# Expert down matrices loaded with two or three neighbouring rows for each partition, in a two-layer decoder trunk

## The chip, the cores and the metric

One core of one Trainium2 chip. The metric is the device time of one execution in microseconds, lower is better; the kernel is timed several times and the median is shown.

## The reference

A trunk of two layers on 256 tokens of width 1024, all in fp32. Layer 0 has differential attention beside a short convolution, then a dense SwiGLU; layer 1 has a gated spatial mix, then experts. Only the experts matter here: each token goes to the two of eight experts that its router picks.

```python
def moe_swiglu(h, router_w, w1, w3, w2):
    ...
    logits = jnp.einsum('nd,de->ne', xt, router_w, preferred_element_type=jnp.float32)
    top_val, top_idx = lax.top_k(logits, TOP_K)
    gates = jax.nn.softmax(top_val, axis=-1)
    ...
        return (jax.nn.silu(xb @ w1[e]) * (xb @ w3[e])) @ w2[e]
    ...
    contrib = y_sorted * gate_flat[order][:, None].astype(h.dtype)
    out = jax.ops.segment_sum(contrib, sorted_token, num_segments=n_tok)
```

`w1[e]` and `w3[e]` are 1024 x 2816 (the up matrices), `w2[e]` is 2816 x 1024 (the down matrix). All eight experts' matrices are read once: 277 MB of the 358 MB that the kernel reads.

## The kernel before

**Weights.** `Stream` brings every weight matrix through one chain, in one order. SP issues loads into raw tiles of 128 partitions x 3072 fp32 (1536 KB, 12 KB for each partition); in the expert stage there are seven (`RAWA` + `RAWB`). `convert` then splits each raw tile, mostly 1536 columns at a time: ACT rounds it to `whi` (L153) and DVE takes the rest, `wlo = raw - whi` (L154). There are four pairs of these conversion buffers. TensorE (PE) multiplies from them: a product is `whi` and `wlo` each against the activations. Once both halves of a raw tile are converted, the next load may go into it. `prefetch` issues loads as soon as a raw tile can be had, so SP waits for DVE to be done with L154.

**What a load looks like.** `rows` packs blocks of 128 matrix rows into raw tiles, and `piece` writes the source of a load of m blocks as `(k p) f -> p k f`: partition p gets row p of each block, so its m rows lie 128 rows apart in the matrix, and each is a run of 4 KB for a width of 1024.

**An expert step.** For each expert the 2816 hidden columns go in three steps (`MAIN`: 1024, 1024 and 768 wide). `up` multiplies the gathered tokens with the step's columns of `w1` and `w3`. Then the hidden values, which lie with tokens on the partitions, must be turned so that hidden columns lie on the partitions, in blocks of 128. `down` multiplies block j with the rows of `w2` of that block; it is held back by one step, so that it runs beside the next step's `up`.

- Experts in the places 0, 2, 4, 6 hold up to 128 tokens ("large"). `up` leaves the product in `g`, written by DVE in two halves (L1160), and `turn` transposes it block by block (L1195): each transpose loads 128 columns of `g` into PE as weights and streams the identity, out to `gTp`.
- Experts in the places 1, 3, 5, 7 hold up to 64 ("small"): the rounded tokens sit in 64 lanes and their remainders in the other 64. `up` leaves two tiles `ab`, for `w1` and `w3`, written by ACT in two halves (L1151). `folded` turns a block and adds both lanes at once (L1175): it loads 128 columns of `ab` as weights and streams `fold`, 64 columns; fp32 matmuls of this kind run in two passes. Silu and product come after.

**Order.** On ACT and DVE the order of the expert stage is written out in the program; on PE a scheduler interleaves `down`, transposes, folds and the next `up`.

In the functions below, `g` is what `up` returned, `s` the step, `ctxs[e]["small"]` tells the two kinds apart. `set_aside` loads one raw tile's three blocks as three loads into spare buffers, before the stage has its seven tiles. A second stream (`st2`, `stream.fixed`) serves tokens over an expert's room; its loads bring one block each, and it doesn't run here.

Of the kernel before, what the change touches and what calls it, by code (L numbers as in the profile page):

```python
# [21 lines left out]
P = 128  # L22
D = 1024
# [3 lines left out]
HALF = 64  # L27
# [13 lines left out]
def first_of(parts):  # L41
    return parts[0][0]


def wide(parts):
    return sum(w for _, w in parts)


class Stream:
# [3 lines left out]
    def __init__(self, nc, raws, cvs, cols=RAWC, fixed=None):  # L53
        self.nc, self.raws, self.cvs, self.cols, self.fixed = nc, raws, cvs, cols, fixed
        self.specs, self.loaded, self.n_load = [], [], 0
        self.chunks, self.ready, self.n_conv = [], [], 0
        self.cur, self.pos, self.n_use = None, 0, 0
        self.spare = {}
        self.base, self.ahead, self.parts, self.stop = 0, len(cvs), 1, None

    def add(self, parts, lens):
        i = len(self.specs)
        self.specs.append(parts)
        off = 0
        for n in lens:
            self.chunks.append((i, off, n))
            off += n

    def rows(self, units, cut=0):


        total = sum(u[3] for u in units)
        room = total % self.cols or self.cols
        i = 0
        while i < len(units):
            j, n = i, 0
            while j < len(units) and n < room:
                n += units[j][3]
                j += 1
            assert n == room  # L80
            parts, off, a = [], 0, i
            while a < j:
                b = a + 1
                while b < j and units[b][0] is units[a][0] and units[b][2:] == units[a][2:] \
                        and units[b][1] == units[b - 1][1] + 1:
                    b += 1
                w, k, c0, n1 = units[a]
                parts.append((off, n1, b - a, self.piece(w, k, b - a, c0, n1)))
                off += n1 * (b - a)
                a = b  # L90
            m, q, u = -(-room // CVC), room // 512, 512
            if cut and j == len(units):
                m = cut
            if room % 512:
                q, u = room // 384, 384
            self.add(parts, [(q // m + (x < q % m)) * u for x in range(m)])
            i, room = j, self.cols

    @staticmethod
    def piece(w, k, m, c0, n):  # L100

        return lambda: (w() if callable(w) else w)[k * P:(k + m) * P, c0:c0 + n].rearrange("(k p) f -> p k f", p=P)

    def slab(self, w, s):
        n = SLICES[s]
# [68 lines left out]
def decoder_trunk(ctx: ExitStack, tc: tile.TileContext, x, p, positions, ln_mix, ln_ffn, ln_ple, a_w_in,  # L174
                  a_lambda, a_subln, a_conv_w, a_w_out, ffn_w1, ffn_w3, ffn_w2, c_w_in, c_ln_g, c_ln_b,
                  c_w_s, c_b_s, c_w_out, router_w, moe_w1, moe_w3, moe_w2, ple_gate, ple_proj, final_norm,
                  out, stop=None):
    nc = tc.nc
    V, S, T, G = nc.vector, nc.scalar, nc.tensor, nc.gpsimd
# [15 lines left out]
    def t4(shape=(P, 1024), dt=F32, name="t4"):  # L195
        if name in fixed:
            return fixed[name]
        return t4p.tile(list(shape), dt, tag="t4", name=name)
# [6 lines left out]
    def bank(name="bank", g="B"):  # L205
        return psp.tile([P, 512], F32, tag="bank" + g, name=name)
# [21 lines left out]
    st = Stream(nc, [(rawp, RAWA)], [cvp] * CVA + [cvp2] * CVB)  # L228
# [22 lines left out]
    def at_place(w, i):  # L251

        if i == 0:
            return w[0, 0]
        return lambda: w[0][bass.ds(place[i], 1)].rearrange("o a b -> (o a) b")

    m1, m3, m2 = [[at_place(w, i) for i in range(NE)] for w in (moe_w1, moe_w3, moe_w2)]

    beside = []

# [68 lines left out]
    fold = cst.tile([P, HALF], F32, name="fold")  # L329
# [4 lines left out]
    ident = cst.tile([P, P], F32, name="ident")  # L334
# [477 lines left out]
    for s in range(NSL):  # L812
# [12 lines left out]
        for i in range(len(ab)):  # L825
            n = min(2, nb - 2 * i)
# [75 lines left out]
    for i in range(4):  # L902
        b = bank("sgp")
# [38 lines left out]
    order = tc.manual_schedule(engines={ET.DVE, ET.Activation, ET.Pool})  # L942
# [63 lines left out]
    b = bank("rk")  # L1006
# [124 lines left out]
    def mtile(name, shape, dt):  # L1131
        return fixed[name] if name in fixed else gp.tile(shape, dt, tag=name, name=name)
# [29 lines left out]
                f()  # L1162
        return both if c["small"] else g

    def folded(g, s, own):


        n = wide(s) // P * HALF
        fs, gt = [], t4((P, 2, 512), name="gt")

        def fold_all():
            for src in g:
                b = bank("gTp")
                for j in range(wide(s) // P):
                    T.matmul(b[:, j * HALF:(j + 1) * HALF], src[:, j * P:(j + 1) * P], fold, start=True, stop=True)  # L1175
                fs.append(b[:, :n])

        def parts():
            t = t4((P, 1, 1024), F32R, "gTo") if own else mtile("gTe", [P, 2, 1024], F32R)
            gv = gt[:, 1, :n].rearrange("p (j c) -> p j c", c=HALF)  # L1180
            tv = t[:, 0, :2 * n].rearrange("p (j i c) -> p i j c", i=2, c=HALF)
            S.activation(tv[:, 0], gv, AF.Copy)
            V.tensor_sub(tv[:, 1], gv, tv[:, 0].bitcast(F32))
            return t

        return [lambda: None, fold_all, lambda: S.activation(gt[:, 0, :n], fs[0], AF.Silu),
                lambda: V.tensor_mul(gt[:, 1, :n], fs[1], gt[:, 0, :n])], parts

    def turn(g, s):
        t = mtile("gTe", [P, 2, 1024], F32R)  # L1190
        for (c0, w) in s:
            c0 -= first_of(s)
            b = bank("gTp")
            for j in range(w // P):
                T.transpose(b[:, j * P:(j + 1) * P], g[:, c0 + j * P:c0 + (j + 1) * P], ident)  # L1195
            S.activation(t[:, 0, c0:c0 + w], b[:, :w], AF.Copy)
            V.tensor_sub(t[:, 1, c0:c0 + w], b[:, :w], t[:, 0, c0:c0 + w].bitcast(F32))
        return t
# [23 lines left out]
    def yevac(c, hf):  # L1222
        t = c["yt", hf] = t4((P, 2, 512), F32R, "y")
        S.activation(t[:, 0], c["y"][hf], AF.Copy, scale=c["gg"])
        V.scalar_tensor_tensor(t[:, 1], c["y"][hf], c["gg"], t[:, 0].bitcast(F32), op0=ALU.mult, op1=ALU.subtract)

    def combine(c, hf):

        t, sl = c["yt", hf], halves()[hf]
        bs = [bank("cb") for _ in range(2)]  # L1230
        for tb, b in enumerate(bs):
            for i in range(2):
                T.matmul(b, c["gs"][:, tb * P:(tb + 1) * P], t[:, i], start=i == 0, stop=i == 1)
        for tb, b in enumerate(bs):
            V.tensor_add(h[:, tb, sl], b, h[:, tb, sl])
# [16 lines left out]
    def experts(steps, rk, stream, ctxs, jobs):  # L1252
        e0, last = steps[0][0], steps[-1][0]
        prev, done = None, None
        for e, s in steps:
            end = (e, s) == steps[-1]
            g = up(ctxs[e], s, stream, [lambda hf=hf, c=done: combine(c, hf) for hf in range(2)] if done else ())
            done = None
            at = (e, [u for x, u in steps if x == e].index(s))
            work = jobs.pop(at, [])  # L1260
            if s is steps[-1][1] and e != last and (e - e0) % 2 == 0:
                gather, gates = prep((e + 1, e + 2)[:last - e], rk, ctxs)
                work = gather + work
                for i, f in enumerate(gates):
                    jobs.setdefault((e + 1 + i, 1), []).append(f)
            own, made = end and not stream.fixed, []
            if ctxs[e]["small"]:
                pre, parts = folded(g, s, own)
                work = pre + ([lambda: made.append(parts())] if own else []) + work
            else:  # L1270
                assert not own
            if prev is not None:
                pe, ps, pt = prev
                down(ctxs[pe], ps, pt, stream, work)
                if ps is steps[-1][1]:
                    done = ctxs.pop(pe)
                    for hf in range(2):
                        yevac(done, hf)
            t = made[0] if made else parts() if ctxs[e]["small"] else turn(g, s)
            prev = (e, s, t)  # L1280
        pe, ps, pt = prev
        if stream.fixed:
            down(ctxs[pe], ps, pt, stream)
            for hf in range(2):
                yevac(ctxs[pe], hf)
                combine(ctxs[pe], hf)
            return
        down(ctxs[pe], ps, pt, stream, (), lambda hf: yevac(ctxs[pe], hf))
        order.__exit__(None, None, None)
        with tc.high_priority(150):  # L1290
            for hf in range(2):
                combine(ctxs[pe], hf)

    ctxs = first(steps, rank)
# [31 lines left out]
    with tc.If(most > 0):  # L1326
# [15 lines left out]
        st = Stream(nc, [], [None], 512, (raws, cvf))  # L1342
# [34 lines left out]
```

## Time and profile before

| | |
|---|---|
| median of three runs | 1202.32 us (1202.1 to 1203.17) |
| the profiled execution | 1201.77 us, span 1199.6 us |
| busy in the span | PE 1157.8 us (97%), DVE 973.7 (81%), ACT 838.4 (70%) |
| HBM read | 358.26 MB, 300 GB/s over the span |
| mean granted clock of TensorE | 0.986 of full speed |

The span runs from the first to the last instruction of the profiled execution; the rest of its time lies around it. PE is the matmul part of TensorE and PEld its weight loads, which overlap the matmuls. Matmuls are pipelined, so a PE that shows as busy is not PE at its peak. The expert stage is the stretch from 460 to 1144 us.

### The profile page before, as it was taken

The numbers are of one execution on the slowest core, as the hardware profiler recorded it, in microseconds if no ns is written. First come the engines' busy times: TensorE is split into PE (matmuls) and PEld (weight loads), VectorE is DVE, ScalarE is ACT, GpSimd is POOL, SyncE is SP. The second block draws the span as 40 slices with busy tenths as digits, with TensorE's granted clock in tenths as the row PEclk, the third lists the DMA queues.
The fourth block names the chain that finished last, engine by engine and source line by source line (L and its number), as shares of the span: only waits on it lengthen the run. The fifth ranks groups of instructions, "written<-read, shape, count | busy, mean of one in ns | idle before, by whom it ended". The sixth has DMA issues, their size and how long they took to land.

```text
span 1199.6 us, 16665 instructions
## 1 busy us (share of the span) xinstructions
PE 1157.8 (97%) x6307; PEld 1002.1 (84%) x6307; DVE 973.7 (81%) x1027; ACT 838.4 (70%) x1010; POOL 38.9 (3%) x80
## 2 busy tenths in 40 slices
PE   7999999999999999999999999999999999999985
PEld 5888899998889888988888977888977888987874
DVE  6667665564676868889999989999989999989983
ACT  5645554454465467789888788887788888788864
POOL 1001000010010000000000000000000000000003
PEclk9999999999999979999999999999999999999998
DMA  9633654386456569899999989999989999989921
GB/s 323 227 121 131 232 186 149 120 308 229 144 191 214 219 232 386 330 346 399 402 409 405 406 300 407 406 409 405 399 326 396 372 410 405 402 334 399 396 109 38
DMA packets 112505, 360.46 MB, mean 300 GB/s; under 512 B 6561, under 2 KB 23073, under 8 KB 112418
## 3 DMA queue, kind: packets, MB, share of 16 engines
q1 hardware_dynamic: 110818, 353.56, 77.7%
q0 software_dynamic: 1600, 5.77, 1.5%
q8 instruction: 51, 0.84, 0.3%
q14 instruction: 36, 0.29, 0.1%
HBM read 358.26 MB, written 1.05 MB: 300 GB/s over the span
## 4 chain that ended last, share of the span: by engine, by line
PE 87%; DVE 7%; issue 2%; ACT 2%; DMA 1%; POOL 0%; SPq 0%; POOLq 0%; DVEq 0%; ACTq 0%
DVE wlo L154 4%; PE a L447 3%; PE y L447 3%; PE a L448 3%; PE a L449 3%; PE b L449 3%; PE b L448 3%; PE b L447 3%; PE y L448 3%; PE y L449 3%; PE b L1145 3%; PE gTp L1175 3%; PE b L1144 3%; PE y L1212 2%; PE y L1211 2%
## 5 line engine op out<-in xcount | busy, mean ns | idle before, releaser
L154 DVE TENSOR_TENSOR wlo<-raw,whi 128x1536 fp32r<-128x1536 f32 (+2 forms) x551 | 770.4, 1447 | 149.1 <-ACT whi L153 147.0
L153 ACT ACTIVATE whi<-raw 128x1536 fp32r<-128x1536 f32 (+2 forms) x551 | 660.5, 1237 | 239.4 <-issue 34.2
L1145 PE MATMUL b<-wlo,xs 128*128 128x512 f32 (+1 forms) x192 | 66.9, 397 | 7.5 <-DVE wlo L154 7.4
L448 PE MATMUL a<-wlo,xg 128*128 128x512 f32 (+1 forms) x192 | 71.9, 375 | 0.0
L449 PE MATMUL a<-whi,xg 128*128 128x512 f32 (+1 forms) x192 | 71.7, 373 | 0.0
L448 PE MATMUL b<-wlo,xg 128*128 128x512 f32 (+1 forms) x192 | 71.2, 371 | 0.0
L449 PE MATMUL b<-whi,xg 128*128 128x512 f32 (+1 forms) x192 | 71.2, 371 | 0.0
L1145 PE MATMUL a<-wlo,xs 128*128 128x512 f32 (+1 forms) x192 | 67.1, 381 | 4.0 <-DVE wlo L154 3.9
L449 PE MATMUL y<-whi,gTe 128*128 128x512 f32 x176 | 68.8, 391 | 0.0
L448 PE MATMUL y<-wlo,gTe 128*128 128x512 f32 x176 | 68.8, 391 | 0.0
L447 PE MATMUL b<-whi,xg 128*128 128x512 f32 (+1 forms) x192 | 68.3, 371 | 0.0
L447 PE MATMUL a<-whi,xg 128*128 128x512 f32 (+1 forms) x192 | 67.7, 378 | 0.0
L447 PE MATMUL y<-whi,gTe 128*128 128x512 f32 x176 | 67.1, 395 | 0.0
L1144 PE MATMUL a<-whi,xs 128*128 128x512 f32 (+1 forms) x192 | 65.9, 374 | 0.0
L1144 PE MATMUL b<-whi,xs 128*128 128x512 f32 (+1 forms) x192 | 63.3, 378 | 0.0
L1212 PE MATMUL y<-wlo,gTe 128*128 128x512 f32 x164 | 58.8, 402 | 0.0
L1211 PE MATMUL y<-whi,gTe 128*128 128x512 f32 x164 | 57.0, 394 | 0.0
L481 PE MATMUL ap<-hTh,whi 128*128 128x256 f32 x176 | 49.8, 284 | 1.4 <-ACT hTh L432 1.4
L482 PE MATMUL ap<-hTl,whi 128*128 128x256 f32 x176 | 49.9, 284 | 0.1
L482 PE MATMUL b3p<-hTl,whi 128*128 128x256 f32 x176 | 49.8, 283 | 0.0
L483 PE MATMUL b3p<-hTh,wlo 128*128 128x256 f32 x176 | 49.8, 283 | 0.0
L481 PE MATMUL b3p<-hTh,whi 128*128 128x256 f32 x176 | 49.8, 283 | 0.0
(357 smaller groups left out, 2357.5 us busy)
## 6 DMA issues: line engine op xcount, KB each, us to landing
raw<-in_moe_w_dram SPq DMA_DIRECT2D x143, 1536.0 KB, 9.9
raw<-in_moe_w_dram SPq DMA_DIRECT2D x32, 1024.0 KB, 9.3
raw<-in_ffn_w_dram SPq DMA_DIRECT2D x19, 1536.0 KB, 6.7
raw<-in_moe_w_dram SPq DMA_DIRECT2D x32, 512.0 KB, 8.7
raw<-in_a_w_in_dram SPq DMA_DIRECT2D x4, 1536.0 KB, 9.3
raw<-in_ple_gate_dram SPq DMA_DIRECT2D x4, 1536.0 KB, 9.9
raw<-in_c_w_in_dram SPq DMA_DIRECT2D x4, 1536.0 KB, 6.5
raw<-in_a_w_in_dram SPq DMA_DIRECT2D x4, 1024.0 KB, 9.5
```

Of the source, the lines that this page charges most:

```text
L153: self.nc.scalar.activation(hi[:, a:b], raw[:, off - base + a:off - base + b], AF.Copy)
L154: self.nc.vector.tensor_sub(lo[:, a:b], raw[:, off - base + a:off - base + b], hi[:, a:b].bitcast(F32))
L447: T.matmul(o, ah, bh, start=first, stop=False, **kw)
L448: T.matmul(o, ah, bl, start=False, stop=False, **kw)
L449: T.matmul(o, al, bh, start=False, stop=last, **kw)
L481: T.matmul(o, a, tr.hi(k), start=first and c % 512 == 0, stop=False, **kw)
L482: T.matmul(o, a, tr.lo(k), start=False, stop=False, **kw)
L483: T.matmul(o, b, tr.hi(k), start=False, stop=last, **kw)
L1144: T.matmul(ob[:, :w], c["x"][0][k], wh, start=k == 0, stop=False)
L1145: T.matmul(ob[:, :w], c["x"][0][k], wl, start=False, stop=k == 7)
L1211: T.matmul(c["y"][hf], th, wh, start=start, stop=False)
L1212: T.matmul(c["y"][hf], th, wl, start=False, stop=end)
```

## The change

A down load of two or three blocks, full width, now asks for `(p k) f -> p k f`: partition p gets rows m\*p to m\*p + m - 1 of the load, one run of 8 or 12 KB. Block i of the load then holds rows i, m + i, 2m + i and so on of the matrix, and the hidden values must be turned in the same order: `turn` and `folded` read 128 columns that lie m apart. `blocks` remembers for each block which load it came with, and `columns` gives the slice. Up matrices, loads of one block, and the last expert's last step (half rows of 512 columns) keep their form. For `st2` there is nothing in `blocks`, so its slices stay as they were.

```diff
@@ Stream.rows
-                parts.append((off, n1, b - a, self.piece(w, k, b - a, c0, n1)))
+                m = 1
+                if n1 == D and any(w is x for x in self.whole):
+                    m = b - a
+                    for i in range(m):
+                        self.blocks[self.whole.index(w), k + i] = (k, m, i)
+                parts.append((off, n1, b - a, self.piece(w, k, b - a, c0, n1, m > 1)))
@@
-    def piece(w, k, m, c0, n):
+    def piece(w, k, m, c0, n, near=False):
...
-        return lambda: (w() if callable(w) else w)[k * P:(k + m) * P, c0:c0 + n].rearrange("(k p) f -> p k f", p=P)
+        order = "(p k) f -> p k f" if near else "(k p) f -> p k f"
+        return lambda: (w() if callable(w) else w)[k * P:(k + m) * P, c0:c0 + n].rearrange(order, p=P)
+
+    def columns(self, e, f):
+
+        k, m, i = self.blocks.get((e, f), (f, 1, 0))
+        return slice(k * P + i, k * P + i + m * (P - 1) + 1, m)
@@
+    st.whole = m2
@@
+    def hidden(stream, e, s, j):
+
+        c = stream.columns(e, first_of(s) // P + j)
+        return slice(c.start - first_of(s), c.stop - first_of(s), c.step)
@@ folded
-                    T.matmul(b[:, j * HALF:(j + 1) * HALF], src[:, j * P:(j + 1) * P], fold, start=True, stop=True)
+                    T.matmul(b[:, j * HALF:(j + 1) * HALF], src[:, hidden(stream, e, s, j)], fold,
+                             start=True, stop=True)
@@ turn
-                T.transpose(b[:, j * P:(j + 1) * P], g[:, c0 + j * P:c0 + (j + 1) * P], ident)
+                T.transpose(b[:, j * P:(j + 1) * P], g[:, hidden(stream, e, s, c0 // P + j)], ident)
```

On SP's queue, in the loads of the first small expert, before (`raw` is the raw tile; the last numbers are partitions x runs x elements of a run):

```order
L126 DMA raw_5239<-in_moe_w3_dram 128x1024
L126 ISA
L126 DMA raw_5239<-in_moe_w2_dram 128x2x1024
L126 ISA
L126 DMA raw_5266<-in_moe_w2_dram 128x3x1024
L126 ISA
L126 DMA raw_5313<-in_moe_w2_dram 128x3x1024
L126 ISA
L126 DMA raw_5353<-in_moe_w1_dram 128x4x768
```

The same place of the changed program:

```order
L139 DMA raw_5239<-in_moe_w3_dram 128x1024
L139 ISA
L139 DMA raw_5239<-in_moe_w2_dram 128x2048
L139 ISA
L139 DMA raw_5266<-in_moe_w2_dram 128x3072
L139 ISA
L139 DMA raw_5313<-in_moe_w2_dram 128x3072
L139 ISA
L139 DMA raw_5353<-in_moe_w1_dram 128x4x768
```

No load moved: the down loads have one run for each partition where they had two or three, in the same place. In the whole program 45 loads have 128x3072 and 16 have 128x2048; the up loads and the 4x768 ones are as before.

On PE, at the folds of a small expert's second tile, before (`y` is the down product of the expert ahead):

```order
L447 MATMUL y<-whi,gTe 128x512
L448 MATMUL y<-wlo,gTe 128x512
L449 MATMUL y<-whi,gTe 128x512
L1175 MATMUL gTp<-fold,ab 128x64 x8
L447 MATMUL y<-whi,gTe 128x512
L448 MATMUL y<-wlo,gTe 128x512
```

The same place of the changed program:

```order
L461 MATMUL y<-whi,gTe 128x512
L462 MATMUL y<-wlo,gTe 128x512
L463 MATMUL y<-whi,gTe 128x512
L1194 MATMUL gTp<-fold,ab 128x64 x2
L461 MATMUL y<-whi,gTe 128x512
L1194 MATMUL gTp<-fold,ab 128x64 x6
L462 MATMUL y<-wlo,gTe 128x512
```

Six of the eight folds stand one down matmul later; this is so in four places of the program, and in a fifth a split of 5 and 3 folds becomes 4 and 4. In expert 0's first step the transposes, which stood as x4, one matmul, x4, stand as x2, two matmuls, x6. All other bursts, and all of ACT, DVE and POOL, keep their order.

## Rows read from the trace of the kernel before

**Rows 1.** Busy time by stretch, 460 to 1144 us; the last columns are clock, DMA share, rate.

```profile
core 0: us, PE busy (x) PEld busy (x) DVE busy (x) ACT busy (x) POOL busy (x), PEclk, DMA share, GB/s
...
605.00:701.00 96.00, 96.00 (x469) 82.58 (x468) 87.53 (x69) 73.22 (x71) 0.00 (x0) 1.00 0.99 391
701.00:784.00 83.00, 79.09 (x407) 66.11 (x406) 80.00 (x57) 73.54 (x72) 0.00 (x0) 1.00 1.00 387
784.00:880.00 96.00, 96.00 (x471) 82.65 (x470) 87.53 (x69) 73.22 (x71) 0.00 (x0) 1.00 0.99 389
880.00:963.00 83.00, 79.10 (x398) 65.97 (x397) 78.54 (x57) 72.06 (x70) 0.00 (x0) 0.98 0.98 380
```

**Rows 2.** Who waited for whom, 460 to 1143 us: us in total, times, longest.

```profile
DVE wlo L154 <- ACT whi L153: 45.3, 68, 4.1
ACT whi L153 <- PE b L449: 23.4, 47, 0.8
ACT whi L153 <- PE y L449: 22.7, 26, 2.4
ACT whi L153 <- PE a L449: 20.7, 30, 2.4
...
PEld a L448 <- DVE wlo L154: 0.2, 1, 0.2
```

**Rows 3.** The raw tiles, 460 to 1143 us: users, idle time before them, landing.

```profile
L154 DVE TENSOR_TENSOR wlo<-raw,whi x335: 1222/1757/1768, 459.5 to 1141.7; 128x1536 fp32r<-128x1536 f32 x167, 128x1024 fp32r<-128x1024 f32 x1
L153 ACT ACTIVATE whi<-raw x334: 1060/1490/1617, 463.8 to 1139.7; 128x1536 fp32r<-128x1536 f32 x166, 128x1024 fp32r<-128x1024 f32 x1
...
its engine sat idle before it (us, times) until:
  ACT whi L153: 44.9, 67
  PE b L449: 23.4, 47
...
DMA to landing us min/median/max: 5.8/9.6/14.0
```

**Rows 4.** SP's own waits, 460 to 1143 us.

```profile
SPq L126 <- DVE wlo L154: 563.9, 166, 8.6
```

**Rows 5.** DMA queues, 592 to 640 us, and then 648 to 660.

```profile
DMA packets 5049, 19.67 MB, mean 410 GB/s; under 512 B 255, under 2 KB 255, under 8 KB 5046
...
DMA packets 1617, 4.82 MB, mean 402 GB/s; under 512 B 48, under 2 KB 48, under 8 KB 1617
```

**Rows 6.** Chain of waits, 784 to 880 us, then 701 to 784: start, us, what.

```profile
811.55 0.87 PE gTp L1195 x8
...
725.65 1.73 PE gTp L1175 x16
```

**Rows 7.** Weight loads of L417, L1175 and L1195: duration in ns, min/median/max.

```profile
L417 PEld LDWEIGHTS rb<-ident,rstd x6: 134/134/135, 27.0 to 358.7; 128*128 128x128 f32 x6
...
L1175 PEld LDWEIGHTS gTp<-fold,ab x352: 186/192/330, 537.8 to 1137.5; 128*128 128x128 f32 x176
...
L1195 PEld LDWEIGHTS gTp<-ident,g x88: 137/140/143, 462.0 to 1062.7; 128*128 128x128 f32 x88
```

**Rows 8.** Timeline of DVE and of PE, 628 to 634 us, a large expert.

```profile
629.58 1.28 DVE L1160 TENSOR_TENSOR g<-b,g 128x512 f32<-128x512 f32 x2
...
631.84 0.39 PE L1211 MATMUL y<-whi,gTe 128*128 128x512 f32 x1
632.07 0.39 PE L1212 MATMUL y<-wlo,gTe 128*128 128x512 f32 x1
...
632.76 1.03 PE L1195 MATMUL gTp<-ident,g 128*128 128x128 f32 x8
```

**Rows 9.** Timeline of ACT and of PE, 720 to 728 us, a small expert.

```profile
721.38 1.07 ACT L1151 ACTIVATE ab<-b 128x512 f32<-128x512 f32 x2
...
725.49 1.89 PE L1175 MATMUL gTp<-fold,ab 128*128 128x64 f32 x16
```

**Rows 10.** Chain of waits, 701 to 784 us: shares by line.

```profile
by line: PE b L1145 12.2%; DVE wlo L154 11.4%; PE gTp L1175 11.2%; PE b L1144 9.3%; PE y L1211 6.9%; PE a L1145 6.9%; PE y L1212 6.6%; PE a L1144 6.5%; issue 5.9%; PE y L447 3.7%; ACT whi L153 3.6%; PE y L449 3.6%; PE y L448 3.6%; DVE h L12
```

More of the change, by code (lines that the diff above doesn't have):

```diff
@@ L59, in __init__ @@
         self.base, self.ahead, self.parts, self.stop = 0, len(cvs), 1, None
+        self.whole, self.blocks = [], {}
     def add(self, parts, lens):
@@ L1163, in up, with folded @@
         return both if c["small"] else g
-    def folded(g, s, own):
+    def hidden(stream, e, s, j):
+        c = stream.columns(e, first_of(s) // P + j)
+        return slice(c.start - first_of(s), c.stop - first_of(s), c.step)
+    def folded(g, s, own, stream, e):
         n = wide(s) // P * HALF
@@ L1187, in folded, with turn @@
                 lambda: V.tensor_mul(gt[:, 1, :n], fs[1], gt[:, 0, :n])], parts
-    def turn(g, s):
+    def turn(g, s, stream, e):
         t = mtile("gTe", [P, 2, 1024], F32R)
@@ L1267, in experts @@
             if ctxs[e]["small"]:
-                pre, parts = folded(g, s, own)
+                pre, parts = folded(g, s, own, stream, e)
                 work = pre + ([lambda: made.append(parts())] if own else []) + work
@@ L1278, in experts @@
                         yevac(done, hf)
-            t = made[0] if made else parts() if ctxs[e]["small"] else turn(g, s)
+            t = made[0] if made else parts() if ctxs[e]["small"] else turn(g, s, stream, e)
             prev = (e, s, t)
```

## The prediction

> **What bounds the kernel now.** The change touches nothing before the expert stage, so I read that stage alone, from 460 us (its first matmuls) to 1144 us (its last): 684 us of the span's 1199.6. I read it in four steps: the busy time by expert, who waits for whom, how far the loads run ahead, and what the transposes and folds cost.
>
> By expert [rows 1]: the stretches alternate. 605 to 701 and 784 to 880 are experts of 128 rows (0, 2, 4, 6), the others mostly the small ones. In the large ones PE is busy for all of 96.0 us and DVE for 87.5. In the small ones (701 to 784) PE is busy for 79.1 of 83 us and DVE for 80.0: two engines almost full, either can set the pace. The DMA queues' share is about 1.0 everywhere, so a reader is tempted to call the stage DMA-bound.
>
> The waits say no. In the view of waits for 460 to 1143 us [rows 2] there are 32 rows, and none names a DMA as the releaser. `whi` (ACT, L153), the first reader of a raw tile, waits for PE to give conversion buffers back (23.4 + 22.7 + 20.7 us and more). The view of the raw tiles [rows 3] says the same: before all 335 conversions, engines sat idle for ACT and PE, never for a landing. The queue itself waits: SP for `wlo` of DVE, 563.9 us in 166 waits [rows 4]; that is, for a raw buffer to be emptied. How far ahead are the loads? The stage moves about 390 GB/s [rows 1], so a tile of 1536 KB passes every 1572864 / 390e3 = 4.0 us, and the seven buffers last 28 us. Of that a load takes 9.6 us from issue to landing [rows 3], and the two conversions of a tile about 5 us (1.49 + 2 x 1.76). Some 13 us are left in which a landed tile just lies there. A full DMA queue here is a symptom of buffers that are refilled at once.
>
> **The change, part by part.** *1. Longer rows in the loads.* By the program's order, 45 loads go from three runs of 4 KB for each partition to one of 12 KB, 16 from two to one of 8 KB; the three single loads into `spare` and the last expert's 512-column ones keep their runs. What this is worth to a queue that is full comes from two windows in which it is: with 4 KB runs 410 GB/s, with 3 KB runs (the 768-column loads) 402 [rows 5]; 19.67 MB in the 4794 packets of over 512 bytes, and 4.82 MB in 1569, are those sizes. For one of 16 engines that is 16 x 4096 / 410e3 = 0.1598 us a run and 16 x 3072 / 402e3 = 0.1223: 0.0375 us for 1024 bytes, and 0.0098 that a run costs whatever its size. A load has 8 partitions for each engine. So a three-row load saves 8 x 2 x 0.0098 = 0.157 us, a two-row one 0.078; together 45 x 0.157 + 16 x 0.078 = 8.3 us of queue time. No run over 4 KB stands in this queue before, so that it stays one transfer is not shown. [...] The rows show 9.8 ns. Either way I put it at nothing on the path: the 13 us of lead hide it, and the queue would have to be over 10 us late in a row before a conversion saw it. With that cover gone it would be worth at most 8.3 us.
>
> *2. Strided columns in the weight loads.* `turn` (88 transposes in the large experts) and `folded` (164 folds in the small ones, each in two passes) now load their 128 columns two or three apart. Counting blocks: 72 transposes at step three and 16 at step two; 132 folds, so 264 loads, at step three, and 32 folds, 64 loads, at step two; 12 folds of the last expert stay. In a burst these loads set the pace: eight transposes take 0.87 us and sixteen fold passes 1.73 [rows 6], 0.109 us each, whereas 64 columns at the pace of the 512-column matmuls (one every 0.23 us, [rows 8]) would pass in 0.03. So whatever a strided load costs more, PE pays. What it costs is not in the trace: every other load is contiguous or repeats one column. From below: nothing. The nearest row is L417, whose 128 columns all come from one address; its load takes 134 ns, against 140 for a contiguous transpose [rows 7]. There the time hangs on the number of columns, not on the bytes under them. From above: as if the columns in between were read too, three times 0.109 us, or +0.218 at step three and +0.109 at step two. I take the end that the nearest row is close to, nothing, and keep the rest for the range.
>
> *3. A block now needs columns of both halves.* Blocks of a three-row load spread over 384 columns, so the third block of a 1024-wide step must wait for the second half of `g` or `ab`, which the order shows as x8 becoming x2, a matmul, x6. This costs nothing where the halves are done long before. In the large expert at 629.58 to 630.86 DVE writes both halves, and the transposes start at 632.76 [rows 8], 1.9 us later; in the small one ACT writes `ab` from 721.38 to 722.45 and the folds start at 725.49 [rows 9], 3.0 us later. Behind them PE would hold the down matmuls. Only expert 0's first step is tighter, and there two matmuls now stand between.
>
> *4. Down matmuls read the same tiles as before*, in another order of rows; count, shape and conversions stay. Shorter access patterns on SP cost or save tenths of a microsecond beside 563.9 us of waiting.
>
> Sum: 1201.77 us (the profiled execution: span 1199.6 and 2.2 around it) + 0 - 0 = 1201.8. The median of the runs shown is 1202.32, 0.55 above; I forecast on that scale, **1202.3 us**.
>
> **The rivals.** *A: no measurable change* (the sum). Its own range is 1200 to 1204.5: the stretch 880 to 963 shows a mean clock of 0.98 [rows 1], 2% of 83 us or 1.7 us that a shifted wait may add or give back. Chance 0.51.
>
> *B: a step of three costs half a load more; slower.* Place: the bursts. If a column three away from the last takes half a step longer, a load takes 0.163 us instead of 0.109, +0.054; step two still free. Large experts: 72 x 0.054 = 3.9 us, all on the path since PE is never idle there. Small ones: 264 x 0.054 = 14.3 us, of which DVE's pace hides between nothing and all; the chain of waits runs through gTp for 11.2% and through wlo for 11.4% of that stretch [rows 10], so I halve it, 7.1. That gives 1202.3 + 11 = 1213, from 1206 to 1220. It decides from about 0.03 us a load on: 72 x 0.03 plus half of 264 x 0.03 is 6 us. Speaks for it: nothing on PE shows such a step to be free. Against: the L417 row. Chance 0.30. [...]
>
> *C: the full upper end.* +0.218 and +0.109: 72 x 0.218 + 16 x 0.109 = 17.4 us in the large experts, and 264 x 0.218 + 64 x 0.109 = 64.5 in the small ones, half to all of it: 1252 to 1284. Chance 0.04.
>
> *D: the queue mattered after all; faster.* If landings end waits that the view put down to PE, the 8.3 us come back, wholly 1194.0, half 1198.2. Against it stand 32 rows of waits without a DMA and the lead of 13 us. Chance 0.13.
>
> *E: the change doesn't do what it says* (long runs are cut again into 4 KB pieces). That is possible, and changes nothing in the time: it lies inside A. The remaining 0.02 are losses from a new wait in part 3.
>
> **How the numbers follow.** The likeliest is A, 1202.3. To hold the time 8 times in 10: all of A (0.51), D down to 1197.5 (about 0.07), B up to 1215 (about 0.21): 1197.5 to 1215. 0.2% of 1202 is 2.4 us, about what a measurement of this kernel can tell from no change. Faster by more: D, 0.13. Slower by more: B, C and the rest, 0.36. Same: 0.51.
>
> **What the profile after would show.** Part 1 right: fewer packets in q1 (45 x 256 + 16 x 128 = 13,568 fewer of 110,818) and a rate above 410 GB/s in stretches of down loads, with the DMA share falling below 1.0 since the buffers set the pace. Part 1's zero right: still no DMA among the releasers. Part 2 right: bursts of eight transposes still 0.87 us, load medians still 140 and 192 ns; wrong: these rows grow, and the large stretches grow from 96 us by the same amount. Part 3 wrong: gTp waiting for `g` or `ab`. The prediction falls if strided loads cost over 0.03 us each, or if tiles are in truth converted as they land.

## The result and the profile after

The changed kernel takes **1218.54 us** (median of 4 runs, 1217.03 to 1219.05) against 1202.23 (also of 4) before: a ratio of 1.0134 [1.0122, 1.0145], 16.3 us slower, where 1202.3 was forecast and the range ended at 1215. The profiled execution has a span of 1216.3 us, 16.7 over the one before, at the same mean granted clock (0.986).

The loads did become what the diff says. From the page of the changed kernel, the DMA totals and the queue of the loads:

```profile
DMA packets 98937, 360.46 MB, mean 296 GB/s; under 512 B 6561, under 2 KB 23073, under 8 KB 91042
...
q1 hardware_dynamic: 97250, 353.56, 76.5%
```

q1 has 97,250 packets where it had 110,818: 13,568 fewer, exactly the 45 x 256 + 16 x 128 that were counted, so a run of 8 or 12 KB stays one transfer.

What the change cost shows first in the waits. Who waited for whom from 460 to 1160 us, changed kernel (us in total, times, longest):

```profile
DVE wlo L167 <- ACT whi L166: 59.5, 82, 4.1
ACT whi L166 <- PE y L463: 25.8, 26, 3.1
ACT whi L166 <- PE b L463: 23.9, 48, 0.8
ACT whi L166 <- PE a L463: 20.6, 30, 2.4
...
ACT whi L166 <- PE b L1158: 16.5, 11, 2.9
...
PEld b L1159 <- DVE wlo L167: 15.8, 25, 2.6
...
ACT whi L166 <- PE y L1231: 14.2, 14, 1.9
...
PE b L1159 <- DVE wlo L167: 7.1, 5, 2.2
PEld a L1159 <- DVE wlo L167: 6.4, 9, 1.2
...
PE a L1159 <- DVE wlo L167: 3.5, 6, 0.8
...
PEld gTp L1194 <- ACT ab L1165: 0.9, 1, 0.9
...
PE gTp L1194 <- ACT ab L1165: 0.5, 1, 0.5
```

Still no PE, ACT or DVE row names a DMA, and SP, in the same view for its own waits, waits longer for a raw buffer than in [rows 4]:

```profile
SPq L139 <- DVE wlo L167: 584.7, 167, 8.7
```

The rows that moved are `whi` waiting for PE and, behind it, `wlo` waiting for `whi` (45.3 us in [rows 2], 59.5 here). So it is PE that gives the conversion buffers back later. Where PE lost the time is seen in the view of the tile `gTp` (duration in ns, min/median/max):

```profile
L1194 PEld LDWEIGHTS gTp<-fold,ab x352: 187/260/331, 538.9 to 1154.2; 128*128 128x128 f32 x176
L1194 PE MATMUL gTp<-fold,ab x352: 217/337/421, 539.1 to 1154.3; 128*128 128x64 f32 x176
L1215 PEld LDWEIGHTS gTp<-ident,g x88: 188/198/218, 462.5 to 1076.6; 128*128 128x128 f32 x88
L1215 PE MATMUL gTp<-ident,g x88: 270/277/389, 462.5 to 1076.7; 128*128 128x128 f32 x88
```

Both loads grew by about 60 ns against [rows 7]: the median of the folds from 192 to 260 ns, that of the transposes from 140 to 198. A record's duration isn't yet a price, though: these records overlap (260 ns of a fold's load against 0.173 us from one fold to the next), and only that distance is paid. The chain of waits shows that (start, us, what), here two bursts (folds or transposes that stand one right behind the other) of folds from 755 to 765 us and one of transposes of the large expert:

```profile
758.86 2.10 PE gTp L1194 x14
...
762.63 2.44 PE gTp L1194 x16
...
821.16 0.92 PE gTp L1215 x8
```

Sixteen folds take 2.44 us where they took 1.73, eight transposes 0.92 where they took 0.87 [rows 6]. The same lengthening of the load record cost the folds 0.71 us in a burst and the transposes 0.05. Summed over the stage, from the start of one pass to the start of whatever follows it on PE, the folds went from 36.9 to 51.4 us (+14.5), the transposes from 8.4 to 9.1 (+0.7). Within bursts the median distance of two folds went from 0.112 us to 0.173. PE's pauses elsewhere grew by 0.6. That is 15.8 of the 16.4 us by which the stage's last matmul starts later (at 1153.0 us before, not at 1144 as the prediction has it, and at 1169.4 after); 0.6 us are left without a place.

### The profile page after: what moved, and what is told of

The parts are those of the page before. It is cut to its first block, busy times and chain, and to the rows that moved or that the text cites. A ratio compares the mean times of both kernels' runs of the same rounds, so it can differ in the third digit from the quotient of the medians.

```text
span 1216.3 us, 16665 instructions
## 1 busy us (share of the span) xinstructions
PE 1174.6 (97%) x6307; PEld 1019.6 (84%) x6307; DVE 975.1 (80%) x1027; ACT 839.4 (69%) x1010; POOL 38.8 (3%) x80
## 3 DMA queue, kind: packets, MB, share of 16 engines
q1 hardware_dynamic: 97250, 353.56, 76.5%
HBM read 358.26 MB, written 1.05 MB: 295 GB/s over the span
## 4 chain that ended last, share of the span: by engine, by line
PE 86%; DVE 7%; issue 3%; ACT 2%; DMA 1%; POOL 0%; SPq 0%; POOLq 0%; DVEq 0%; ACTq 0%
DVE wlo L167 5%; PE gTp L1194 4%; PE a L461 3%; PE a L462 3%; PE y L461 3%; PE a L463 3%; PE y L462 3%; PE b L463 3%; PE b L461 3%; PE b L462 3%; PE y L463 3%; PE b L1159 3%; PE y L1232 3%; PE b L1158 3%; PE y L1231 3%
## 5 line engine op out<-in xcount | busy, mean ns | idle before, releaser
L1194 PEld LDWEIGHTS gTp<-fold,ab 128*128 128x128 f32 x352 | 62.0, 244 | 3.1 <-ACT ab L1165 0.9
L1194 PE MATMUL gTp<-fold,ab 128*128 128x64 f32 x352 | 59.2, 313 | 0.5 <-ACT ab L1165 0.5
```

The costliest lines, as they stand in the source:

```text
L1194: T.matmul(b[:, j * HALF:(j + 1) * HALF], src[:, hidden(stream, e, s, j)], fold, start=True, stop=True)
```

## The experiments

**Which half of the change.** Two kernels take it apart: one keeps the long loads and reads adjacent columns, the other keeps the loads of before and reads with the stride.

```diff
x1_loads_only, in hidden():
-        c = stream.columns(e, first_of(s) // P + j)
-        return slice(c.start - first_of(s), c.stop - first_of(s), c.step)
+        return slice(j * P, (j + 1) * P)
x2_reads_only, in Stream.rows:
-                parts.append((off, n1, b - a, self.piece(w, k, b - a, c0, n1, m > 1)))
+                parts.append((off, n1, b - a, self.piece(w, k, b - a, c0, n1)))
```

> The down loads keep their 8 and 12 KB runs; transposes and folds read adjacent columns again, so hidden columns and rows of the down matrix no longer belong together and the output is not the reference's. Theory 1 (the loss is the weight loads of columns three apart, in the folds): about 1202 us, fold steps back at 0.112 us, DMA packets as in the changed kernel. Theory 2 (the longer runs themselves slow the stage): about 1218 us. Theory 3 (a block now waits for both halves of ab or g): 1202, but see the next run. If faster loads were worth something after all, under 1199.

> The down loads are as before the change, 4 KB runs; transposes and folds read columns two and three apart, so hidden columns and rows no longer belong together and the output is not the reference's. Theory 1: about 1218 us, all of the loss. Theory 2: about 1202. Theory 3: 1218 too, but then with PE idle in front of gTp for ab or g, which theory 1 does not need.

Measured: long loads alone 1202.23 us, ratio 0.9996 [0.9986, 1.0005]; strided reads alone 1218.56, 1.0138 [1.0121, 1.0155]. The whole loss is in the reads, and the queue time that the longer loads save, 8.3 us by the prediction's sum, is worth nothing on the path. The tile `gTp` of the two kernels, x1 first:

```profile
L1193 PEld LDWEIGHTS gTp<-fold,ab x352: 186/192/335, 539.5 to 1140.8; 128*128 128x128 f32 x176
```

```profile
L1194 PEld LDWEIGHTS gTp<-fold,ab x352: 188/260/332, 538.3 to 1153.6; 128*128 128x128 f32 x176
```

The load's record follows the stride (192 with adjacent columns, 260 with strided ones) whatever the DMA did.

**Which reads.** Two more kernels change only the large experts (transposes) or only the small ones (folds).

```diff
-    st.whole = m2
+    st.whole = [w if i not in SMALL else None for i, w in enumerate(m2)]   # x3_large_only
+    st.whole = [w if i in SMALL else None for i, w in enumerate(m2)]       # x4_small_only
```

> Long runs and strided columns only in the large experts (places 0, 2, 4, 6), that is transposes alone. Theory 1 by the steps of the changed kernel's trace: 88 transposes dearer by 0.007 us, 0.6 us, so 1202 to 1203.5. Had the transposes cost what the folds do, 72 x 0.063 = 4.5 us, 1207. Theory 2 with half of the long runs: about 1210.

> Long runs and strided columns only in the small experts (places 1, 3, 5, 7), that is folds alone. Theory 1: 264 loads dearer by 0.063 us and 64 by 0.006, 17.0 us, all on the path: about 1218. If DVE's pace hid half of them, 1210. Theory 2 with half of the long runs: about 1210.

Measured: large only 1203.24, 1.0007 [0.9997, 1.0017]; small only 1216.99, 1.0124 [1.0107, 1.0141]. Against the 1202.06 of the kernel before beside them, the folds cost 14.9 us; the 1.2 of the transposes aren't clear of no change. In the large-only kernel the load of the transposes has its longer record all the same:

```profile
L1215 PEld LDWEIGHTS gTp<-ident,g x88: 190/198/218, 462.4 to 1063.9; 128*128 128x128 f32 x88
```

So 88 loads that last 58 ns longer (5.1 us) are almost free there. A fold's matmul has 64 columns, a transpose's 128, and the distance of two transposes was 0.109 us before and 0.114 after: their pace is set by something else than the load. That it is their own columns, under which the load would pass, is the first guess; the next experiment speaks against it.

**By distance or not?** If the price is one of distance, the time grows with the distance of two columns. If not, it may stop growing from some step on. This kernel keeps the loads of before (by the edit of x2) and reads with steps of four, eight and six columns in the three hidden steps of an expert.

```diff
-        c = stream.columns(e, first_of(s) // P + j)
-        return slice(c.start - first_of(s), c.stop - first_of(s), c.step)
+        if wide(s) == 768:
+            a, b = j, 6
+        elif first_of(s) == 0:
+            a, b = j // 4 * 512 + j % 4, 4
+        else:
+            a, b = j, 8
+        return slice(a, a + b * (P - 1) + 1, b)
```

> Only for the price of a step: loads as before the change, and transposes and folds read columns four apart in an expert's first hidden step, eight apart in its second and six apart in its third; hidden columns and rows no longer belong together, so the output is not the reference's. [...] Price by distance (each column more costs 0.063 us): 0.24, 0.36 and 0.49, and about 1290 us. For the transposes: 0.109 to 0.12 if they stay cheap as in the changed kernel, 0.22 if a load of twice the time reaches their pace.

Measured in one execution: 1254.38 us. The chain of waits from 545 to 615 us has a burst at each step: four at 548.61, eight at 573.29, six at 601.90.

```profile
548.61 3.56 PE gTp L1199 x16
...
573.29 3.71 PE gTp L1199 x16
...
601.90 2.55 PE gTp L1199 x12
```

Sixteen folds take 3.56 us at step four and 3.71 at step eight; twelve take 2.55 at step six. From start to start that is 0.233, 0.238 and 0.222 us at the median, about twice the 0.112 of adjacent columns and nearly alike: from step four on the price doesn't grow. Distance is out. Twice the 0.112 us for each of the 352 loads adds 39 us to the 1202.0 of the kernel before beside it, an estimate of 1241; the total is 13 us above that. Of the 52 us by which the last matmul is later, the folds hold 38 and the transposes 1.0; pauses and slower passes in stretches with TensorE's granted clock at half of full speed (41 us of the stage; 7 in the kernel before, where it is 0.50 from 928 to 931 us) hold about 15 more than before, and the pauses elsewhere shrank by about 2. The windows show that the granted clock was lower than in [rows 1] (last three columns: clock, DMA share, rate):

```profile
701.00:784.00 83.00, 79.72 (x341) 66.71 (x340) 64.09 (x46) 58.05 (x66) 0.00 (x0) 0.92 0.88 336
880.00:963.00 83.00, 79.69 (x367) 67.65 (x366) 69.39 (x53) 63.44 (x70) 0.00 (x0) 0.96 0.90 338
```

With the 0.118 us of step two (below) the row for the folds is 0.112, 0.118, 0.173 and 0.22 to 0.24 us at steps of one, two, three and four or more: 1, 1.05, 1.54 and 1.98 to 2.13 times. Three columns apart cost a fold's load 0.061 us more, about half of it, and four 0.121, a whole one. Why the row has this form is not shown.

The transposes don't follow this row. The chain of waits of the same kernel, 784 to 890 us, has a burst at step four and one at step eight:

```profile
837.29 0.95 PE gTp L1220 x8
...
874.40 0.89 PE gTp L1220 x8
```

Eight transposes take 0.95 and 0.89 us where they took 0.87 [rows 6]; over the stage the median distance is 0.113 us. A new load passes every 0.11 to 0.13 us there, at steps at which a fold's load takes 0.22 to 0.24. Loads of 0.22 us one behind the other don't fit into that, whatever the columns of a transpose may cover: there the stride itself costs little. What sets the two apart (a transpose runs in one pass, 88 records for 88, a fold in two, 352 for 176) wasn't tried.

**Step two everywhere.** The loads (by the edit of x2) and PE's order of before, all reads two columns apart.

```diff
-        c = stream.columns(e, first_of(s) // P + j)
-        return slice(c.start - first_of(s), c.stop - first_of(s), c.step)
+        a = j // 2 * 2 * P + j % 2
+        return slice(a, a + 2 * (P - 1) + 1, 2)
```

> Loads as before the change, order of PE as before the change; all transposes and folds read columns two apart, in pairs of blocks; hidden columns and rows no longer belong together, so the output is not the reference's. Price of a step of two alone: 352 fold passes dearer by 0.006 us and 88 transposes by 0.007, 2.7 us, so 1204 to 1205.5.

Measured: 1206.56, 1.0037 [1.0025, 1.005]. The tile's load, then the chain of waits at two bursts:

```profile
L1194 PEld LDWEIGHTS gTp<-fold,ab x352: 193/196/335, 537.7 to 1141.3; 128*128 128x128 f32 x176
```

```profile
726.16 1.82 PE gTp L1194 x16
...
814.03 0.95 PE gTp L1215 x8
```

Sixteen folds take 1.82 us (1.73 with adjacent columns, 2.44 mostly with step three). Over the stage folds cost 2.0 us more than before and transposes 1.0; the granted clock falls once more (at 750.3 us; 0.98 from 701 to 784 us, 1.00 in [rows 1]), which can hold the rest, 1.4 of the 4.4 us. So step two isn't quite free, 0.006 us a load of the folds, and the measured time is 1 us above the upper end expected.

**Loads of at most two blocks.** If three is the dear step, a change that stops at two should lose little. A first kernel let blocks 5 to 7 stay together, 48 passes at step three:

```diff
                         and units[b][1] == units[b - 1][1] + 1 \
+                        and not (b - a == 2 and units[a][3] == D and units[a][1] != 5
+                                 and any(units[a][0] is x for x in self.whole)):
```

> The changed kernel with its three-row loads split into a load of two rows and one of one, so that no column lies three apart (expert 0's tile that goes to the spare buffers keeps its three, in transposes). Theory 1 with the step of two that the changed kernel's trace shows (0.118 against 0.112 us): about 250 fold loads dearer by 0.006, 1.5 us, so 1203 to 1204.5. If any step but one is dear and only the burst's place hid it: 1210 to 1218.

Measured: 1213.82, 1.0084 [1.0055, 1.0113]. Its stretches of small experts show the granted clock lower than [rows 1] (0.96), so the number mixes the 48 dear passes, the clock and a changed order on PE, and decides nothing:

```profile
701.00:784.00 83.00, 78.38 (x380) 65.61 (x379) 75.36 (x54) 68.88 (x68) 0.00 (x0) 0.96 0.94 361
```

The second splits all of them but one load of expert 0:

```diff
+                        and not (b - a == 2 and units[a][3] == D
+                                 and any(units[a][0] is x for x in self.whole[units[a][1] == 5:])):
```

> The changed kernel with every three-row load split into one of two rows and one of one (the run before had left the third load of every expert whole, by a slip), so that nothing but expert 0's spare tile has a step of three. Theory 1: folds at 0.118 and 0.112 us, some 1.5 us over before, so 1203 to 1205. If the splitting itself, which also changes PE's order in some places, costs something of its own: 1207 to 1212, with PE idle elsewhere than in the folds.

Measured: 1208.58, 1.0046 [1.0029, 1.0063]. The folds are back to 1.3 us over before, the transposes to 0.7:

```profile
L1196 PEld LDWEIGHTS gTp<-fold,ab x352: 188/196/331, 538.7 to 1144.7; 128*128 128x128 f32 x176
```

But PE's pauses elsewhere are 3.9 us longer than before, and there are waits that the kernel before doesn't have (waits, 460 to 1150 us):

```profile
PEld a L1160 <- ACT whi L168: 2.4, 2, 1.2
...
PE a L1160 <- ACT whi L168: 1.6, 2, 0.8
DVE wlo L169 <- DMA raw<-in_moe_w_dram: 1.6, 2, 1.2
```

So the second of the two expectations came true. Splitting the loads shifts PE's order in several places and makes conversions wait for a landing twice. Which of the shifts costs the 3.9 us wasn't tried.

**Why nothing was hidden.** In the small experts DVE is nearly as full as PE, so I had let half of the loss hide behind it. One theory why it didn't: while PE folds it gives back no conversion buffer, so ACT and DVE stop too. Then one more pair of buffers should hide part of it. To make room, both kernels give up one raw tile of seven.

```diff
-RAWA, RAWB = 4, 3
+RAWA, RAWB = 4, 2
...
+    cvp3 = ctx.enter_context(tc.tile_pool(name="cvp3", bufs=1, reuse_waits="tile"))
-    st.raws, st.cvs, st.base, st.parts = [(rawp, RAWA), (rawp2, RAWB)], [cvp] * CVA, moe_tile, 1
+    st.raws, st.cvs, st.base, st.parts = [(rawp, RAWA), (rawp2, RAWB)], [cvp] * CVA + [cvp3], moe_tile, 1
...
-    st.stop, st.ahead = None, CVA - 1
+    st.stop, st.ahead = None, CVA
...
-    st.ahead = CVA
+    st.ahead = CVA + 1
```

> The kernel before with a fifth pair of conversion buffers in the expert stage, taken from the raw tiles (six instead of seven). Why the small experts hid none of the folds: while PE is in a burst it gives back no conversion buffer, ACT and DVE stop once all four pairs are full, and afterwards DVE is behind. If so, a fifth pair lets DVE go on 1.7 us longer in each burst: 1194 to 1199. If the order of work alone sets it, 1202. If the loads' lead of about 13 us was not real, six raw tiles make it slower, 1206 or more.

> The changed kernel with the same fifth pair of conversion buffers and six raw tiles. If full conversion buffers are what puts the whole price of the dearer folds on the path, a good part of the 16 us comes back: 1202 to 1212. If PE's own work is the pace in the small experts whatever the buffers, 1217 to 1219.

Measured: the kernel before with five pairs 1201.11, 0.9989 [0.9979, 0.9999], 0.9 us faster where the theory asked for 3 to 8; the changed one 1213.81, 1.0088 [1.007, 1.0105], between the ranges of the two theories. That is 4.7 us back of the 16.3. In the waits of the changed kernel with five pairs (460 to 1160 us), PE's waits for `wlo` are about half of those above:

```profile
PEld b L1161 <- DVE wlo L167: 8.7, 15, 0.9
PEld a L1161 <- DVE wlo L167: 5.9, 10, 1.0
...
PE b L1161 <- DVE wlo L167: 3.4, 6, 0.6
...
PE a L1161 <- DVE wlo L167: 2.9, 4, 0.7
```

But they are so in the kernel before with five pairs too, and there the down product has a wait that the changed kernel hardly has (waits of both, the changed one second):

```profile
PEld b L1147 <- DVE wlo L154: 8.6, 15, 0.9
...
PEld y L1214 <- DVE wlo L154: 5.6, 12, 0.6
```

```profile
PEld y L1234 <- DVE wlo L167: 0.9, 4, 0.2
```

So the shorter waits come with the pair in either kernel, and they are not what hides the folds. What one pair more hides is the difference of the differences: the folds still cost 14.8 us more than in the five-pair kernel before, the times lie 12.7 apart instead of 16.3, and 3.6 us are hidden. The wait of `y`, 4.7 us shorter, may be where; that is argued, not shown. Most of the loss isn't hidden with one pair more either, so the buffers are at most a part of the reason. What a second pair more would do wasn't tried. The only kernel here that is ahead of the one before by more than its interval is that one with five pairs, by 0.1%.

## Why the prediction was wrong

**Part 1, the longer loads: right.** The packet count fits to the unit, nothing is gained on the path (x1), and no engine waits for a landing. A load lands in 8.8 us at the median instead of 9.6 [rows 3], but the longer loads aren't the main reason for that. From the views of the raw tiles of the changed kernel, of x1 (long loads alone) and of x2 (strided reads alone):

```profile
DMA to landing us min/median/max: 4.4/8.8/13.2
```

```profile
DMA to landing us min/median/max: 5.0/9.1/13.8
```

```profile
DMA to landing us min/median/max: 4.7/8.8/12.4
```

The slower readers alone, with the loads of before, bring the landing to 8.8; the longer loads alone bring it to 9.1, and SP's wait for a free buffer from 563.9 to 570.3 us.

The rate above 410 GB/s, which I had named as a sign, is there, but small: x1 moves 415 GB/s from 620 to 644 us where the kernel before moves 408. **D** is out: x1 has the faster queue and none of the time back.

**Part 2, the strided loads: this step failed.** "I take the end that the nearest row is close to, nothing." The runs show 0.061 us for a fold's load at step three and 0.006 at step two, 14.5 us over the stage, in its place. The nearest row was L417 [rows 7], whose 128 columns come from one address. It shows that a load of few bytes is hardly faster (134 ns against 140); I read it as if it showed that a load spread over many bytes isn't slower. Reading one place again and again can't show what reading new places costs, and that is what a stride adds: a step of three goes through three times the bytes. L417 is a transpose besides, and the pace of transposes hardly follows the step (0.109 us adjacent, 0.113 in x6). With the bounds 0 and +0.218 us and no row between them, the middle deserved more than 0.30.

**Rival B had the place and almost the size:** half a load at step three, nothing at step two. No run from before the result shows the half load that its +0.054 us starts from; in its place the runs showed +0.061 between folds in a burst, and 0.006 at step two. Its total of 1213 has two wrong terms that cancel in part. "Large experts: 72 x 0.054 = 3.9 us" is 0.7: the sentence that the loads set the pace in a burst holds for the folds alone. And "so I halve it, 7.1" is wrong: all of the folds' loss is on the path. Without the halving, 14.3 us of folds stand against 14.5 measured. The measured 14.5 is less than 264 x 0.061 = 16.1 plus 64 x 0.006 = 0.4, since the first load of each of some 40 bursts lies under a long matmul ahead: that first distance is 0.055 us in both kernels.

Why the halving failed is argued from the waits; the five pairs bear it out only in part. DVE's full share in [rows 1] looked like a second bound that could absorb PE's delay. But DVE and ACT don't run on freely while PE folds. They wait for buffers that only PE's products free: the rows of `whi` waiting for PE sum to 88.5 us before (the three of [rows 2], and 13.2, 6.4 and 2.1 for L1144 and L1211) and to 103.1 after. They fall behind with PE, and PE's waits for `wlo` barely shrink: 16.6 + 7.7 + 7.4 + 3.9 = 35.6 us before, 15.8 + 6.4 + 7.1 + 3.5 = 32.8 in the four rows of the result (sums to compare, not lost time: a wait of PEld can lie under a matmul). The rows of before:

```profile
PEld b L1145 <- DVE wlo L154: 16.6, 27, 2.6
...
PEld a L1145 <- DVE wlo L154: 7.7, 11, 1.2
PE b L1145 <- DVE wlo L154: 7.4, 6, 2.2
...
PE a L1145 <- DVE wlo L154: 3.9, 6, 0.8
```

The windows say the same, here a small stretch of the changed kernel:

```profile
701.00:784.00 83.00, 79.10 (x382) 66.55 (x381) 75.39 (x54) 68.83 (x72) 0.00 (x0) 0.98 0.92 352
```

PE is busy for 79.10 us of the 83 as in [rows 1], though with 382 matmuls instead of 407; DVE is busy for 75.39 instead of 80.00, with 54 operations instead of 57. (The experts have moved against the clock by then, so the two stretches aren't the same work to the matmul.)

**Part 3, blocks of both halves: right.** The only waits of `gTp` for `ab` are the two short rows shown, 0.9 and 0.5 us (0.6 and 0.2 before), and x3, which has the reordered transposes, is within 0.2% of before. **Part 4: right**, no sign of it. **C**, the full upper end, is out: steps of four or more cost a fold's load about 0.12 us, and step three half of that.

## What to carry to other kernels

Here a layout that saved 13,568 packets in a DMA moved its disorder to the reads of the hidden values, and cost 16.3 us: count such reads before the packets, and look at whether the reader or the queue is the bound. A price that no row shows needs a row on the same side of the question; the 134 ns at a step of zero said nothing on a step of three (+0.061 us). And an engine that is 96% busy need not hide another's delay if it waits for the buffers which that other one frees: here it hid nothing, and 3.6 of 16.3 us with one pair more.

## What the runs showed of the hardware

- Weight loads of 128 fp32 columns in a burst of folds (64 columns streamed, two passes): 0.112 us from one to the next with adjacent columns, 0.118 two apart, 0.173 three apart, 0.22 to 0.24 at four, six and eight.
- The same in a burst of fp32 transposes (128 columns streamed, one pass): 0.109 us with adjacent columns, 0.114 with the steps of the changed kernel, 0.113 at four to eight.
- The record of a weight load can grow by 58 ns (140 to 198) while the distance of two loads grows by 5 (0.109 to 0.114 us), as in the transposes. The time follows the distances: in x3 the 88 longer records, 5.1 us by their duration, came with 1.2 us, not clear of no change.
- Runs of 8 and 12 KB for each partition stay one transfer each: q1 had 13,568 packets fewer.
- The granted clock in the small experts differed from kernel to kernel: mean 0.98 to 1.00 in the stretches of [rows 1], 0.92 and 0.96 at steps of four to eight, 0.96 with pairs in x5. What sets these falls is open.
